# A two-layer hybrid decoder trunk: work between weight units issued behind the weight splits, and one tile per PSUM bank

## The chip, the cores and the metric

The kernel runs on one core of one Trainium2 chip. The metric is device time in microseconds of one execution of the whole kernel, the median of three runs. Float32 is the type of all data; TensorE works on pairs of reduced-precision float32 operands, as told below.

## What is computed

Two layers act on a sequence of 256 positions with 2048 channels. The first has a combined input projection that feeds a state-space mixer (a causal convolution of four taps, a chunked scan over 32 heads) and a block attention with 16 heads; the second has a diagonal complex state-space mixer with a gated linear unit. Cut to the parts that matter here:

```python
# layer 0
z, xbc, dt, q, k, v, gate = jnp.split(x @ w_in, SPLITS0, axis=-1)
xbc = jax.nn.silu(causal_depthwise_conv(xbc, conv_w, conv_b))      # 4 taps
y   = ssd_chunked_scan(xh * dt[..., None], dt * a, b, c) + d_skip * xh
y_a = rms_norm(y * jax.nn.silu(z), norm_g)
y_b = moba_attention(rotary(q), rotary(k), v) * jax.nn.silu(gate)
h   = jnp.concatenate([y_a, y_b], axis=-1) @ w_out
# layer 1
u, gate = jnp.split(x @ w_in, 2, axis=-1)
y  = jax.nn.gelu(s5_ssm(u, ...))                                   # complex diagonal recurrence
ga, gb = jnp.split(y @ w_glu, 2, axis=-1)
h  = (ga * jax.nn.sigmoid(gb) * jax.nn.silu(gate)) @ w_out
# both layers
x  = layer_norm(alpha * x + h, g, b)
```

## The kernel before

**Weight units.** All weights are read from HBM as 432 units of 128 x 1024 float32 (512 KB each), in one order for the whole kernel. For each unit `split_to` loads `raw` on SyncE's queue (line 227), ScalarE copies it to the high part `wh` (line 230), and VectorE subtracts that from `raw` for the low part `wl` (line 232). These two instructions are called the split here. The pool that holds `raw`, `wh` and `wl` has four buffers of each, so the split of a unit can start when TensorE has done with the unit four places earlier. `product` calls `split_to(unit[0] + 3)` ahead of a unit's matmuls, so a split is traced three units ahead of its use.

**Products.** A product is eight units (sixteen for the output projection of layer 0), accumulated into two PSUM banks. Each float32 product is three matmuls: high by high, high by low, low by high. `wmm` (line 284) has the weights stationary and leaves a transposed result, 24 matmuls of 256 columns for a unit; `xmm` (line 271) has the activations stationary, 12 matmuls of 512 columns for a unit. `banks()` (line 261) makes one tile of 128 x 2 x 512 that spans both banks, under one of two tags in turn; `Pair` is a list of the two halves that also keeps the whole as `both`. So the banks of a product are used again two products later. In the last unit of a product the first bank is finished before the second.

**Jobs.** What isn't a matmul by weights is cut into small functions. `jobs` holds those that follow a product at once (they read its banks), `back` a long list that is spread over many products. `pump` runs behind each unit's matmuls: it takes as many of `jobs` as are needed to be through by the end of the product, and those of `back` that are due by a rate. `drain` and `finish` run all that is left. Jobs issue on ScalarE, VectorE, TensorE and GpSimd as they need.

**Order on the engines.** The kernel's text gives a trace order only. A scheduler with a model of time then puts the instructions of every engine into a fixed order: at each step an engine takes the instruction with the earliest place in the trace among those that are ready. On the chip each engine runs its own queue strictly in that order and waits at the head of it. A job that was traced much later can so stand ahead of work that was traced earlier, if it was ready sooner in that model. `tc.issue_after(ins)` adds an edge that keeps what is traced inside it, on the engine of `ins`, behind `ins` in that engine's queue. It is an edge of order only, with no wait for `ins` to end. In the kernel before, it is used at two places: `y_split` (line 181) and the steps of the norm between the layers (lines 1002 and 1023).

**Jobs that the prediction follows.**
- `conv_jobs` (line 492): after a product that is to be convolved, four jobs `tap(f)`. Each is one ScalarE instruction (line 498) and three dependent VectorE instructions (line 501) that read the product's bank `f // 2`; a fifth job is a Silu (line 506).
- `trig_job` and `table_job` (lines 544 and 571): about 70 small VectorE instructions that prepare the coefficients of layer 1, traced in the product ahead of the second convolved product of the x columns. `phasor_job` (line 610) works on GpSimd.
- `block_jobs` (line 633): `bars`, `efs`, `pes` and `mts` for each of 16 blocks of layer 1, members of `back`, traced during the attention and the output projection. `bars` issues a load of `bc` on SyncE's queue (line 639) and begins with lines 645 to 651 on VectorE; `efs` has lines 665 to 675.
- `rope_jobs` (line 832): per bank one ScalarE copy (line 838) and VectorE products (lines 839 to 841).
- `product_apart` (line 323): the last product of a layer. Its last units are first accumulated into bank 0 alone, then `after` queues the jobs that read bank 0 (`res0`, line 960, or `res1`, line 1248), then the same units are accumulated into bank 1.
- `ssm(b)` (line 1079): for each of 16 blocks `enc` (TensorE), `rec1` (VectorE, lines 1113 to 1121), `rec2` (VectorE, a scan at line 1128 to line 1131), `dec` (TensorE, lines 1144 and 1148) and `act` (ScalarE), one stage in each step of `back`.
- `gate` (line 1212) in the gated linear unit and the Silu at line 1198, which read both banks by one instruction through `both`.

Of the kernel before, what the change touches and what calls it, by code (L numbers as in the profile page):

```python
# [9 lines left out]
F32 = mybir.dt.float32  # L10
F32R = mybir.dt.float32r
AF = mybir.ActivationFunctionType
OP = mybir.AluOpType
# [3 lines left out]
P = 128  # L17
# [17 lines left out]

SLOT = np.array([[8 * (q // 4) + 4 * (q % 2) + 2 * ((q // 2 % 2) ^ h) + q // 2 % 2 for q in range(64)] for h in range(2)])
GORDER = [16 * h + p + 8 * i for h in range(8) for p in range(8) for i in range(2)]

class Pair(list):
    def __init__(self, both, parts):  # L40
        super().__init__(parts)
        self.both = both


CONST = {}
PARAM = {}
# [118 lines left out]
def trunk(tc, io, out):  # L165
    nc = tc.nc
    V, A, G, T = nc.vector, nc.scalar, nc.gpsimd, nc.tensor
    count = [0]

    def nm(s):  # L170
        count[0] += 1
        return f"{s}_{count[0]}"

    with ExitStack() as top:
# [4 lines left out]
        main = enter(tc.tile_pool(name="main", bufs=1, space=PSUM))  # L179
# [18 lines left out]
        def big(tag, shape, dt=F32):  # L198
            return slot.tile(shape, dt, tag=tag, name=nm(tag))
# [4 lines left out]
        ready = {}  # L204
        nsplit = [0]
        early = {}
        last = {}
        keep = [None, range(0)]

        def split_to(i):  # L210
            while nsplit[0] <= min(i, len(units) - 1):
                n = nsplit[0]
                if n in early:
                    early.pop(n)()
                raw = st.tile([P, UK, 512], F32, tag="raw", name=nm("raw"))
                if n == 0:
                    wh = st.tile([P, UK, 512], F32R, tag="wh", name=nm("wh"))
                    wl = st.tile([P, UK, 512], F32R, tag="wl", name=nm("wl"))
                    for k in range(UK):
                        xpart(k)  # L220
                        nc.sync.dma_start(raw[:, k, :], units[n][:, k * 512 : k * 512 + 512])
                        A.activation(wh[:, k, :], raw[:, k, :], AF.Copy)
                        V.tensor_tensor(wl[:, k, :], raw[:, k, :], wh[:, k, :].bitcast(F32), op=OP.subtract)
                    ready[n] = (wh, wl)
                    nsplit[0] += 1
                    continue
                nc.sync.dma_start(raw.rearrange("p k n -> p (k n)"), units[n])
                pool, th, tl = (keep[0], f"wh{n % 8}", f"wl{n % 8}") if n in keep[1] else (st, "wh", "wl")
                wh = pool.tile([P, UK, 512], F32R, tag=th, name=nm("wh"))
                last["a"] = A.activation(wh, raw, AF.Copy)  # L230
                wl = pool.tile([P, UK, 512], F32R, tag=tl, name=nm("wl"))
                last["v"] = V.tensor_tensor(wl, raw, wh.bitcast(F32), op=OP.subtract)  # L232
                ready[n] = (wh, wl)
                nsplit[0] += 1

        jobs = deque()
        back = deque()
        goal = [0, 0.0]
        unit = [0]
        turnno = [0]  # L240

        def pump(left):
            n = -(-len(jobs) // max(left, 1))
            for _ in range(n):
                jobs.popleft()()
            if back:
                goal[1] += len(back) / max(goal[0] - unit[0], 1)
            while back and goal[1] >= 1.0:
                back.popleft()()
                goal[1] -= 1.0  # L250

        def drain():
            while jobs:
                jobs.popleft()()

        def finish():
            while back:
                back.popleft()()
            goal[1] = 0.0

        def banks():
            turnno[0] += 1
            both = main.tile([P, 2, 512], F32, tag=f"m{turnno[0] % 2}", name=nm("main"))
            return Pair(both, [both[:, o, :] for o in range(2)])

        def xmm(ps, o, wpair, j, hk, start, stop):
            (xh, xl), k = hk
# [20 lines left out]
        def product(kind, hl, nu=CU, prelude=None):  # L288
            ps = banks()
            for u in range(nu):  # L290
                if prelude:
                    prelude(u)
                split_to(unit[0] + 3)
                wpair = ready.pop(unit[0])
                if kind == "w":
                    wmm(ps, u, nu, hl, wpair)
                else:
                    last = u == nu - 1
                    steps = [(j, o) for o in range(2) for j in range(UK)] if last else [(j, o) for j in range(UK) for o in range(2)]
                    for j, o in steps:  # L300
                        xmm(ps, o, wpair, j, hl(u * UK + j), u == 0 and j == 0, last and j == UK - 1)
                unit[0] += 1
                pump(nu - 1 - u)
            return ps
# [68 lines left out]
        with ExitStack() as l0:  # L373
# [3 lines left out]
            def a4(shape, dt=F32):  # L377
                return wk.tile(shape, dt, tag="a4", bufs=6, name=nm("a4"))
# [22 lines left out]
            def xpart(k):  # L401
                xr = a4([P, S])
                nc.sync.dma_start(xr, io["xt"][:, k, :])
                A.activation(xh[:, k, :], xr, AF.Copy)
                V.tensor_tensor(xl[:, k, :], xr, xh[:, k, :].bitcast(F32), op=OP.subtract)
# [104 lines left out]
            ps = product("w", xhl)  # L510
# [3 lines left out]
            ps = product("w", xhl)  # L514
# [217 lines left out]
            for j in range(4):  # L732
                ps = product("w", xhl)
# [84 lines left out]
            for j in range(4):  # L818
                ps = product("w", xhl)
                for i in range(2):  # L820
                    fs = slice(4 * j + 2 * i, 4 * j + 2 * i + 2)
# [85 lines left out]
            for g in range(4):  # L907
                ps = product("w", xhl)
                qT = a4([P, 4, S])
                rope_jobs(ps, qT)  # L910
                ps = product("w", xhl)
                kT = a4([P, 4, S])
                rope_jobs(ps, kT)
                ps = product("x", xhl)
                v = a4([P, 2, 512])
# [8 lines left out]
                ps = product("w", xhl)  # L924
# [38 lines left out]
            ps = product("x", mixhl, 2 * CU, prelude=lambda u: drain() if u == 4 else None)  # L963
            x1[0] = big("D", [P, 2, D])
            jobs.append(lambda ps=ps: res0(a4([P, 2, 512]), ps, 0, (0, 1)))
            for j in range(1, 3):
                ps = product("x", mixhl, 2 * CU)
# [76 lines left out]
        with ExitStack() as l1:  # L1044
# [8 lines left out]
            y5 = {}  # L1053
# [121 lines left out]
            def y_split(j):  # L1175
                if j == 0:
                    y5["h"] = big("A", [P, KT, S], F32R)
                    y5["l"] = big("B", [P, KT, S], F32R)
                yt = y5[j]
                fs = slice(4 * j, 4 * j + 4)  # L1180
                with tc.issue_after(last["a"].ins), tc.issue_after(last["v"].ins):
                    A.activation(y5["h"][:, fs, :], yt, AF.Copy)
                    V.tensor_tensor(y5["l"][:, fs, :], yt, y5["h"][:, fs, :].bitcast(F32), op=OP.subtract)

            for b in range(16):
                ssm(b)
# [5 lines left out]
            sg1 = wk.tile([P, 2, D], F32, tag="sg1", bufs=1, name="sg1")  # L1192
            for j in range(8):
                ps = product("w" if j < 4 else "x", x1hl) if j else first1
                if j < 4:
                    jobs.append(lambda ps=ps, j=j: u_store(ps, j))
                else:
                    jobs.append(lambda ps=ps, j=j: A.activation(sg1[:, :, 512 * j - 2048 : 512 * j - 1536], ps.both, AF.Silu))
                if j == 0:
                    back.extend([lambda fs=fs: [f() for f in fs] for t, fs in sorted(steps.items())])  # L1200
                    goal[0] = unit[0] + 7*CU+10
# [7 lines left out]
            def glu_jobs(ps, j):  # L1209
                d = {}  # L1210

                def gate():
                    sb = w1("gt", [P, 2, 256])
                    A.activation(sb, ps.both[:, :, 256:512], AF.Sigmoid)
                    t1 = d["t"] = w1("p1", [P, 2, 256])
                    V.tensor_tensor(t1, ps.both[:, :, 0:256], sb, op=OP.mult)
                    V.tensor_tensor(t1, t1, sg1[:, :, 256 * j : 256 * j + 256], op=OP.mult)

                def turn():
                    px = sp.tile([P, 2, 512], F32, tag=("enc", "dec")[j % 2], name=nm("turn"))[:, 0, :]  # L1220
                    transpose4(px, [d["t"][:, o, f * P : f * P + P] for f in range(2) for o in range(2)])
                    pv = px.rearrange("p (f s c) -> p f s c", f=2, s=4)
                    ho, lo = (y[:, 2 * j : 2 * j + 2, :].rearrange("p f (c s) -> p f s c", s=4) for y in (y2h, y2l))
                    A.activation(ho, pv, AF.Copy)
                    V.tensor_tensor(lo, pv, ho.bitcast(F32), op=OP.subtract)

                rest = lambda: None
                jobs.extend([gate, rest, rest, turn])
# [5 lines left out]
            for j in range(2, 8):  # L1234
                ps = product("x", y5hl)
# [3 lines left out]
        with ExitStack() as l2:  # L1239
# [11 lines left out]
            for j in range(3):  # L1251
                ps = product("x", y2hl, prelude=lambda u: split_to(unit[0] + 3 + u) if j == 2 else None) if j else first2
# [45 lines left out]
```

## Time and profile before

| | us |
|---|---|
| median of three runs (lowest, highest) | 1376.59 (1375.08, 1376.98) |
| the profiled execution, its time | 1375.91 |
| its span, first to last instruction | 1374.1 |
| mean granted TensorE clock in it | 0.992 of full speed |

The lines of the profile show one execution. Times are in microseconds from the start of the span unless marked ns. PE is TensorE's matmuls, DVE VectorE, ACT ScalarE, POOL GpSimd, SP SyncE. A line such as `L284` is a line of the kernel. In a timeline a row gives the start, the duration, the engine, the line, the operation, the tile written and the tiles read with their shapes, the number of instructions merged into the row, and in brackets how long the engine sat idle before it and which instruction ended that. In the answer on waits a row reads: who waited, for whom, the total, how many times, the longest. In the answer on windows a row gives a stretch, its length, the busy time of each engine with its instructions, the granted clock, the share of DMA time and GB/s.

### The profile page before, as it was taken

The numbers are of one execution on the slowest core, as the hardware profiler recorded it, in microseconds if no ns is written. First come the engines' busy times: TensorE is split into PE (matmuls) and PEld (weight loads), VectorE is DVE, ScalarE is ACT, GpSimd is POOL, SyncE is SP. The second block draws the span as 40 slices with busy tenths as digits, with TensorE's granted clock in tenths as the row PEclk, the third lists the DMA queues.
The fourth block names the chain that finished last, engine by engine and source line by source line (L and its number), as shares of the span: only waits on it lengthen the run. The fifth ranks groups of instructions, "written<-read, shape, count | busy, mean of one in ns | idle before, by whom it ended". The sixth has DMA issues, their size and how long they took to land.

```text
span 1374.1 us, 24912 instructions
## 1 busy us (share of the span) xinstructions
PE 1346.6 (98%) x9944; PEld 1214.5 (88%) x9944; DVE 979.9 (71%) x1548; ACT 673.7 (49%) x856; POOL 307.1 (22%) x457
## 2 busy tenths in 40 slices
PE   9996999999999999999999999899999999999996
PEld 9996999998999999999988888799977788888885
DVE  5789768888666679688768855748888846555555
ACT  5563557765554454454464434344344545444441
POOL 0157787833002002002000000023343200000001
PEclk9998999999999999999999999999999999999998
DMA  8554766555556656646756678387988766666761
GB/s 307 175 162 132 229 195 189 162 181 154 168 162 193 217 164 213 223 150 220 243 175 222 218 219 302 120 305 237 297 278 306 216 211 190 185 192 190 247 216 74
DMA packets 79204, 283.01 MB, mean 206 GB/s; under 512 B 9840, under 2 KB 10480, under 8 KB 78576
## 3 DMA queue, kind: packets, MB, share of 16 engines
q1 hardware_dynamic: 68112, 239.33, 55.4%
q0 software_dynamic: 10400, 40.90, 9.0%
q8 instruction: 78, 1.28, 0.4%
q10 hardware_dynamic: 576, 1.18, 0.2%
q14 instruction: 38, 0.31, 0.1%
HBM read 260.41 MB, written 20.97 MB: 205 GB/s over the span
## 4 chain that ended last, share of the span: by engine, by line
PE 91%; DVE 3%; DMA 2%; POOL 2%; ACT 1%; issue 1%; POOLq 0%; SPq 0%; DVEq 0%; ACTq 0%
PE main L271 42%; PE main L284 41%; DVE wl L232 1%; PE aux L351 1%; PE enc L1103 1%; PE aux L781 1%; DMA raw<-in_wo 1%; PE aux L687 1%; DMA raw<-in_wi 1%; PE aux L359 1%; DMA xr<-in_xn 1%; PE dec L1148 1%; POOL ew L461 1%; PE aux L683 1%; PE aux L861 1%
## 5 line engine op out<-in xcount | busy, mean ns | idle before, releaser
L232 DVE TENSOR_TENSOR wl<-raw,wh 128x1024 fp32r<-128x1024 f32 x431 | 540.7, 1259 | 281.2 <-ACT wh L230 275.2
L230 ACT ACTIVATE wh<-raw 128x1024 fp32r<-128x1024 f32 x431 | 455.4, 1059 | 549.4 <-PE main L271 272.5
L284 PE MATMUL main<-A,wh 128*128 128x256 f32 x1408 | 404.0, 287 | 10.3 <-DVE a L501 10.3
L284 PE MATMUL main<-A,wl 128*128 128x256 f32 x1408 | 400.8, 285 | 0.0
L284 PE MATMUL main<-B,wh 128*128 128x256 f32 x1408 | 400.2, 284 | 0.0
L284 PEld LDWEIGHTS main<-A,wh 128*128 128x128 f32 x1408 | 271.5, 193 | 11.2 <-issue 10.7
L284 PEld LDWEIGHTS main<-B,wh 128*128 128x128 f32 x1408 | 271.5, 193 | 0.3
L284 PEld LDWEIGHTS main<-A,wl 128*128 128x128 f32 x1408 | 271.5, 193 | 0.1
L271 PE MATMUL main<-wh,A 128*128 128x512 f32 x512 | 201.2, 393 | 1.7 <-DVE D L960 1.7
L271 PE MATMUL main<-wl,A 128*128 128x512 f32 x512 | 200.0, 391 | 0.0
L271 PE MATMUL main<-wh,B 128*128 128x512 f32 x512 | 199.6, 390 | 0.0
L271 PE MATMUL main<-wh,C 128*128 128x512 f32 x384 | 152.7, 398 | 0.8 <-DVE D L1248 0.8
L271 PE MATMUL main<-wl,C 128*128 128x512 f32 x384 | 149.9, 390 | 0.0
L271 PE MATMUL main<-wh,F 128*128 128x512 f32 x384 | 149.7, 390 | 0.0
L271 PEld LDWEIGHTS main<-wh,A 128*128 128x128 f32 x512 | 96.1, 188 | 22.2 <-DVE D L960 2.1
L271 PEld LDWEIGHTS main<-wh,B 128*128 128x128 f32 x512 | 96.1, 188 | 20.0
L271 PEld LDWEIGHTS main<-wl,A 128*128 128x128 f32 x512 | 96.2, 188 | 19.2
L271 PEld LDWEIGHTS main<-wh,C 128*128 128x128 f32 x384 | 72.1, 188 | 16.8 <-DVE D L1248 1.2
L271 PEld LDWEIGHTS main<-wh,F 128*128 128x128 f32 x384 | 72.1, 188 | 15.2
L271 PEld LDWEIGHTS main<-wl,C 128*128 128x128 f32 x384 | 72.1, 188 | 14.2
L284 PE MATMUL main<-C,wh 128*128 128x256 f32 x256 | 74.1, 290 | 0.7 <-ACT C L1014 0.7
L284 PE MATMUL main<-F,wh 128*128 128x256 f32 x256 | 73.5, 287 | 0.3 <-DVE F L1015 0.3
(281 smaller groups left out, 1575.6 us busy)
## 6 DMA issues: line engine op xcount, KB each, us to landing
raw<-in_wi SPq DMA_DIRECT2D x271, 512.0 KB, 4.2
raw<-in_wo SPq DMA_DIRECT2D x96, 512.0 KB, 4.2
raw<-in_wglu SPq DMA_DIRECT2D x64, 512.0 KB, 3.7
wt<-wb POOLq DMA_DIRECT2D x16, 896.0 KB, 7.7
wb<-ob POOLq DMA_DIRECT2D x16, 512.0 KB, 5.8
bc<-in_s5bc SPq DMA_DIRECT2D x16, 256.0 KB, 4.3
wb<-F POOLq DMA_DIRECT2D x16, 256.0 KB, 4.0
wb<-om POOLq DMA_DIRECT2D x16, 128.0 KB, 4.3
```

Of the source, the lines that this page charges most:

```text
L230: last["a"] = A.activation(wh, raw, AF.Copy)
L232: last["v"] = V.tensor_tensor(wl, raw, wh.bitcast(F32), op=OP.subtract)
L271: T.matmul(ps[o], l[:, k, sl], r[:, j, :], start=start and i == 0, stop=stop and i == 2)
L284: T.matmul(pv[o // 2][:, o % 2, :], l[:, j, sl], r[:, k, :], start=first and i == 0 and o % 2 == 0, stop=end and i == 2 and o % 2 == 1, sk ...
L351: T.transpose(dst[:, i * P : i * P + P], s, ident)
L359: T.matmul(px[:64, 0:64], idle, idle, start=i == 0, stop=i == n - 1)
L461: G.tensor_scalar(pl, pl, 1.0 / (2 * k + 1), None, op0=OP.add)
L683: T.transpose(pe[:, a * P : a * P + P], ev[:, a, :], ident)
L687: T.matmul(pk[at : at + 64, a * 16 : a * 16 + 16], ev[:, a, 64 * i : 64 * i + 64], cv[:, a, i, :], start=True, stop=True)
L781: T.matmul(yo, xs[:, 0, xc], df[:, i, 0:256], start=True, stop=False)
L861: T.matmul(px[:, 128:384], qT[:, h, P:S], kT[:, h, :], start=True, stop=True)
L1103: T.matmul(px[64 * at : 64 * at + 64, i, r * 128 + q * 64 : r * 128 + q * 64 + 64], wt[64 * i : 64 * i + 64, a * P + 64 * r : a * P + 64 * ...
```

## The change

Every job is now run through a new function `run`, which opens an `issue_after` edge to the two split instructions of one unit before it calls the job. At the time of `pump` behind a unit, `unit[0]` is already that unit plus one, so the split is that of the third unit ahead of the one whose matmuls were just traced, or the last one split if there is none so far ahead. All ScalarE and VectorE instructions of the job stand behind it in their queues. Instructions on TensorE, GpSimd and SyncE get no edge. The special edge in `y_split` goes. `split_to` keeps the two instructions of every unit in `splits`.

The second part: `banks()` makes two tiles of one bank each in place of one tile of two banks, and the class `Pair` goes. The two kinds of instruction that read both banks at once are therefore cut in two: the Silu of the gate columns in layer 1 (four products) and the Sigmoid and the first product of `gate` (eight products).

```diff
-                last["a"] = A.activation(wh, raw, AF.Copy)
+                high = A.activation(wh, raw, AF.Copy)
                 wl = pool.tile([P, UK, 512], F32R, tag=tl, name=nm("wl"))
-                last["v"] = V.tensor_tensor(wl, raw, wh.bitcast(F32), op=OP.subtract)
+                splits[n] = (high, V.tensor_tensor(wl, raw, wh.bitcast(F32), op=OP.subtract))
...
+        def run(job):
+            with ExitStack() as pin:
+                for ins in splits.get(min(unit[0] + 2, nsplit[0] - 1), ()):
+                    pin.enter_context(tc.issue_after(ins.ins))
+                job()
+
         def pump(left):
             n = -(-len(jobs) // max(left, 1))
             for _ in range(n):
-                jobs.popleft()()
+                run(jobs.popleft())
...
-                back.popleft()()
+                run(back.popleft())
...
         def banks():
             turnno[0] += 1
-            both = main.tile([P, 2, 512], F32, tag=f"m{turnno[0] % 2}", name=nm("main"))
-            return Pair(both, [both[:, o, :] for o in range(2)])
+            return [main.tile([P, 512], F32, tag=f"m{turnno[0] % 2}{o}", name=nm("main")) for o in range(2)]
...
-                with tc.issue_after(last["a"].ins), tc.issue_after(last["v"].ins):
-                    A.activation(y5["h"][:, fs, :], yt, AF.Copy)
-                    V.tensor_tensor(y5["l"][:, fs, :], yt, y5["h"][:, fs, :].bitcast(F32), op=OP.subtract)
+                A.activation(y5["h"][:, fs, :], yt, AF.Copy)
+                V.tensor_tensor(y5["l"][:, fs, :], yt, y5["h"][:, fs, :].bitcast(F32), op=OP.subtract)
...
-                    jobs.append(lambda ps=ps, j=j: A.activation(sg1[:, :, 512 * j - 2048 : 512 * j - 1536], ps.both, AF.Silu))
+                    jobs.append(lambda ps=ps, j=j: [A.activation(sg1[:, t, 512 * j - 2048 : 512 * j - 1536], ps[t], AF.Silu) for t in range(2)])
...
-                    A.activation(sb, ps.both[:, :, 256:512], AF.Sigmoid)
                     t1 = d["t"] = w1("p1", [P, 2, 256])
-                    V.tensor_tensor(t1, ps.both[:, :, 0:256], sb, op=OP.mult)
+                    for t in range(2):
+                        A.activation(sb[:, t, :], ps[t][:, 256:512], AF.Sigmoid)
+                    for t in range(2):
+                        V.tensor_tensor(t1[:, t, :], ps[t][:, 0:256], sb[:, t, :], op=OP.mult)
                     V.tensor_tensor(t1, t1, sg1[:, :, 256 * j : 256 * j + 256], op=OP.mult)
```

`drain` and `finish` go through `run` in the same way.

More of the change, by code (lines that the diff above doesn't have):

```diff
@@ L37 @@
 GORDER = [16 * h + p + 8 * i for h in range(8) for p in range(8) for i in range(2)]
[L39 to L42, printed above, removed]
 CONST = {}
@@ L206, in trunk @@
         early = {}
-        last = {}
+        splits = {}
         keep = [None, range(0)]
@@ L253, in drain @@
             while jobs:
-                jobs.popleft()()
+                run(jobs.popleft())
         def finish():
             while back:
-                back.popleft()()
+                run(back.popleft())
             goal[1] = 0.0
```

## The prediction

> **What bounds the kernel now.** I read the shares of busy time first, then TensorE's waits, then the stretch in which its longest wait lies.
>
> ```profile
> span 1374.1 us, 24912 instructions
> ...
> PE 1346.6 (98%) x9944; PEld 1214.5 (88%) x9944; DVE 979.9 (71%) x1548; ACT 673.7 (49%) x856; POOL 307.1 (22%) x457
> ```
>
> TensorE is the bound, and it has 1374.1 - 1346.6 = 27.5 us without work. A change that adds and removes no matmul can win only from these and from a lowered clock, or lose by adding to them. So the answer on TensorE's waits comes next.
>
> ```profile
> PE main L284 <- DVE a L501: 10.3, 1, 10.3
> PE main L271 <- DVE D L960: 1.7, 1, 1.7
> ...
> PE main L271 <- DVE D L1248: 0.8, 1, 0.8
> ```
>
> One wait of 10.3 us is the largest item. No wait for a split (`wl` L232) is in that answer: no split is late for TensorE today, so putting splits first wins nothing by itself. The long wait, in the timeline and in windows of all engines (PE, PEld, DVE, ACT, POOL busy; then the clock):
>
> ```profile
> 109.24 0.28 PE L284 MATMUL main<-A,wl 128*128 128x256 f32 x1
> 119.86 0.55 PE L284 MATMUL main<-A,wh 128*128 128x256 f32 x1 [10.34 <-DVE a L501]
> ```
>
> ```profile
> 92.00:109.20 17.20, 17.20 (x146) 17.20 (x145) 16.18 (x41) 9.89 (x15) 10.59 (x20) 1.00 0.51 154
> 109.20:119.90 10.70, 0.36 (x4) 0.19 (x2) 10.70 (x24) 1.62 (x3) 7.31 (x11) 0.73 0.52 161
> 119.90:130.20 10.30, 10.30 (x70) 10.30 (x71) 9.70 (x28) 5.71 (x7) 9.17 (x24) 0.79 0.09 38
> 130.20:148.00 17.80, 17.80 (x152) 17.80 (x151) 15.36 (x31) 8.96 (x11) 13.65 (x26) 1.00 0.63 193
> ```
>
> At 109.24 the third convolved product of the x columns cannot begin, since VectorE still reads the banks of the first (the last `tap`). VectorE is full: 10.70 of 10.70 us. The clock is low behind the wait too: 0.79 over 10.3 us costs 10.3 x 0.21 = 2.2 us. Wait and clock together: 12.5 us.
>
> **The ties.** What VectorE does in that wait:
>
> ```profile
> 108.71 0.73 DVE L645 TENSOR_TENSOR bb<-bc,wri 128x128 f32<-128x128 f32 x1
> 109.37 0.61 DVE L647 SCALAR_TENSOR_TENSOR bb<-bc,consts,wri 128x128 f32<-128x128 f32 x1
> ...
> 115.01 0.28 DVE L646 TENSOR_TENSOR tm<-bc,wri 128x128 f32<-128x128 f32 x1
> 115.22 0.34 DVE L648 SCALAR_TENSOR_TENSOR tm<-bc,consts,wri 128x128 f32<-128x128 f32 x1
> 115.48 0.47 DVE L501 SCALAR_TENSOR_TENSOR a<-main,params,a 128x255 f32<-128x255 f32 x1
> ...
> 118.47 0.60 DVE L665 TENSOR_TENSOR et<-bb,lam 128x128 f32<-128x128 f32 x2
> ...
> 119.03 0.38 DVE L666 TENSOR_TENSOR tm<-bb,lam 128x128 f32<-128x128 f32 x1
> 119.25 0.46 DVE L501 SCALAR_TENSOR_TENSOR a<-main,params,a 128x253 f32<-128x253 f32 x1
> ...
> 144.91 0.36 DVE L646 TENSOR_TENSOR tm<-bc,wri 128x128 f32<-128x128 f32 x1 [2.40 <-DMA bc<-in_s5bc]
> ```
>
> L645 to L666 are `bars` and `efs` of the first S5 block. They were traced during the attention, long after the taps, and stand here because their inputs were ready. Behind the tie they follow a split of the attention and leave this stretch. The six rows shown ahead of the last tap are 0.73 + 0.61 + 0.28 + 0.34 + 0.60 + 0.38 = 2.9 us. In the whole stretch (windows of the instructions on tile `bc`, then on `et`, two sets without overlap):
>
> ```profile
> 92.00:148.00 56.00, 4.92 (x12) 0.91 0.47 147
> ```
>
> ```profile
> 92.00:148.00 56.00, 0.00 (x0) 0.00 (x0) 1.70 (x5) 0.91 0.47 147
> ```
>
> So 6.6 us of VectorE's work goes, and the 2.40 us at 144.91 in which a block's instruction at the head of the queue waited for its DMA. Both come back during the attention and the output projection, beside matmuls, with no bank to hold up. The load of `bc` has no edge (SyncE), but its buffer comes free with `efs`, so it moves with the ties; raw loads stand behind it on that queue, with four buffers of raw weights as cover.
>
> **The banks.** The waits of 1.7 and 0.8 us are in `product_apart`: the matmul that waits writes bank 1, the VectorE instruction that it waits for (L960, L1248) reads bank 0. They share only the two-bank tile. With a tile for each bank both waits go: 1.7 + 0.8 = 2.5 us. What follows hangs on the end of bank 1's matmuls and moves up with them. The same dependency strings the taps together:
>
> ```profile
> 97.92 0.56 ACT L498 ACTIVATE a<-main,params 128x256 f32<-128x256 f32 x1 [1.15 <-DVE a L501]
> ...
> 104.35 0.56 ACT L498 ACTIVATE a<-main,params 128x256 f32<-128x256 f32 x1 [2.44 <-DVE a L501]
> ...
> 110.87 0.56 ACT L498 ACTIVATE a<-main,params 128x256 f32<-128x256 f32 x1 [3.20 <-DVE a L501]
> ```
>
> These begin taps 1, 2 and 3. Tap 2 reads the other bank and yet waits 2.44 us for tap 1's VectorE work. With two tiles taps 2 and 3 can run beside tap 1, and can start up to 104.35 - 97.92 = 6.4 us earlier.
>
> How much of the 12.5 us goes? At least 2.9 (the rows ahead of the last tap, clock still lowered); at most all 12.5. For the value I count VectorE's load. It was busy 16.18 + 10.70 + 9.70 + 15.36 = 51.9 us from 92 to 148; less 6.6 that is 45.3. TensorE without wait and low clock takes 56 - 12.5 = 43.5 us for its part. VectorE is then 1.8 us short, and 17.20 - 16.18 = 1.0 us of idle in the first window waits for ScalarE and stays: 2.8. Since the order in the queue won't be the best, I take a stall of 4 us, by the next taps or by a split that is now late, in one piece or several. In this trace the clock fell about 5 us into the wait (0.73 over 10.7 us is 5.8 us at half speed), so 4 us leaves it up. Win: 12.5 - 4 = 8.5 us.
>
> By "What's actually happening" in "TensorE: Matmul & The Clock Gate" of the Trainium skill the clock halves after one idle window of about 3.4 us; by that, an unbroken 4 us could still cost what it costs now, and the win would be 6.3.
>
> **What is added.** One instruction on both banks becomes two, by these groups (count | busy us, mean ns):
>
> ```profile
> L1198 ACT ACTIVATE sg<-main 128x1024 f32<-128x1024 f32 x4 | 4.1, 1028 | 0.0
> L1214 ACT ACTIVATE gt<-main 128x512 f32<-128x512 f32 x8 | 4.6, 580 | 0.0
> L1216 DVE TENSOR_TENSOR p<-main,gt 128x512 f32<-128x512 f32 x8 | 5.5, 684 | 0.7 <-ACT gt L1214 0.7
> ...
> L498 ACT ACTIVATE a<-main,params 128x256 f32<-128x256 f32 x24 | 13.4, 558 | 20.6 <-DVE a L501 20.5
> L501 DVE SCALAR_TENSOR_TENSOR a<-main,params,a 128x255 f32<-128x255 f32 (+2 forms) x72 | 34.1, 474 | 1.6 <-ACT a L498 0.5
> ```
>
> Silu: 4 x (2 x 0.580 - 1.028) = 0.5 us. Sigmoid: 8 x (2 x 0.558 - 0.580) = 4.3 us. Product: 8 x (2 x 0.474 - 0.684) = 2.1 us. Beside them:
>
> ```profile
> 1150.00:1285.00 135.00, 135.00 (x610) 111.74 (x610) 73.25 (x67) 60.20 (x61) 1.09 (x2) 1.00 0.65 204
> ```
>
> VectorE and ScalarE are about half idle there while matmuls fill all 135 us, so the cost is nothing; without that cover it is 6.9 us.
>
> **The sum.** 2.5 + 8.5 = 11.0 us. The profiled execution's 1375.91 would be 1364.9; it lies 0.7 under the median 1376.59, so I forecast 1376.59 - 11.0 = 1365.6 us. Its own range, the stall that is left between 1 and 8 us: 1362 to 1370.
>
> **What the ties can cost.** A tied job stands behind a split that waits for a weight buffer, and so do all jobs behind it. The nearest chain back to TensorE is in layer 1, where `dec` needs `rec2`:
>
> ```profile
> 961.34 1.27 DVE L1128 TENSOR_TENSOR_SCAN gt<-rt,p 128x256 f32<-128x256 f32 x2
> ...
> 965.50 0.42 DVE L1131 SCALAR_TENSOR_TENSOR gt<-p,p 128x256 f32<-128x256 f32 x1
> ...
> 969.13 1.23 DVE L232 TENSOR_TENSOR wl<-raw,wh 128x1024 fp32r<-128x1024 f32 x1 [2.08 <-ACT wh L230]
> ...
> 972.72 1.28 DVE L1113 TENSOR_TENSOR p<-enc,wt 128x512 f32<-128x512 f32 x2
> ```
>
> ```profile
> 974.19 0.34 PE L1144 MATMUL dec<-um,wt 64*64 64x64 f32 x8
> ```
>
> Counted by units, this `rec2` belongs behind the split at 969.13: it starts 9 us later. Today 974.19 - 965.92 = 8.3 us lie between its end and `dec`. Nearly all goes, but `dec` has no edge and is placed where its input is ready, between other matmuls; so I price it at nothing. If its place in TensorE's queue is too early, each block waits.
>
> **The rivals.**
>
> *Slower: the recurrence arrives late.* If the next block's `rec1` (972.72) also goes first, `rec2` begins at 969.13 + 1.2 + 2.1 = 972.4 and ends about 3.5 us of its own work later, 975.9: `dec` would wait 1.7 us. At all 16 blocks that is 27 us; at half of them, 13.6, for slacks and shifts differ: 1365.6 + 13.6 = 1379. It decides from the point at which `rec2` moves more than 8.3 us. For it: VectorE is in order, and 8.3 us is about the shift. Against it: TensorE shows no such wait today.
>
> *Faster by less: VectorE is slowed, not crowded.* It works beside GpSimd's `phasor_job` here, and its small instructions are stretched:
>
> ```profile
> 129.76 1.11 DVE L606 TENSOR_TENSOR a<-lap 128x64 f32<-128x64 f32 x1
> ...
> 135.57 0.27 DVE L606 TENSOR_TENSOR a<-lap 128x64 f32<-128x64 f32 x1
> ```
>
> The same instruction takes 1.11 us at one time and 0.27 at another. If that sets the pace, what the ties clear away is filled by waiting, and only the 2.9 us and the banks' 2.5 are won: 1376.6 - 5.4 = 1371.2. "Who interferes with whom" in "SBUF — State Buffer" of the Trainium skill says that a VectorE instruction with two SBUF inputs and a GpSimd instruction that reads SBUF block each other; by it the stretch stays, since the change moves nothing on GpSimd.
>
> *Nothing.* Dependencies are kept per bank already, and the queues' order is what the model of time makes of VectorE's load either way: 1376.6. Against it stands the wait of tap 2 on tap 1.
>
> **Chances.** Forecast 0.50, faster by less 0.17, nothing 0.08, slower 0.25. So faster by over 0.2% (2.8 us, about what a measurement of this kernel can tell from no change) 0.67, within it 0.08, slower 0.25. The range 1361 to 1381 leaves out the upper half of the slower case and the last of the win.
>
> **What would show it.** Right: no wait for L960 or L1248 in TensorE's waits; no L645 before 400 us; the wait for L501 under 5 us and the clock at 1.00 from 110 to 130 us; tap 2 not waiting for tap 1. Wrong: the wait for L501 still near 10 us, new waits of TensorE for L1131 or L232, or any of several microseconds elsewhere.

## The result and the profile after

| | before | after |
|---|---|---|
| median of 20 runs, us | 1376.64 | 1373.97 |
| lowest and highest | 1374.97, 1379.20 | 1368.98, 1376.19 |
| profiled execution: time, span | 1375.91, 1374.1 | 1374.45, 1372.7 |

The ratio after to before is 0.9979, with a 95% interval of 0.9973 to 0.9985. The kernel is faster by 2.7 us, a quarter of the 11.0 us forecast, and its runs spread over 7.2 us where those of before spread over 4.2. The span and the shares of busy time of the changed kernel:

```profile
span 1372.7 us, 24925 instructions
...
PE 1351.4 (98%) x9944; PEld 1216.5 (89%) x9944; DVE 980.6 (71%) x1556; ACT 673.0 (49%) x868; POOL 296.9 (22%) x457
```

TensorE has 21.3 us without work in place of 27.5, but is busy 4.8 us longer with the same matmuls, though the mean granted clock of the span is 0.992 in both executions. The answer on TensorE's waits (who waited, for whom, total, times, longest):

```profile
PE dec L1147 <- DVE gt L1129: 3.7, 1, 3.7
PE aux L350 <- DVE D L1005: 1.4, 1, 1.4
...
PE main L283 <- DVE a L500: 0.9, 1, 0.9
PE dec L1143 <- ACT ys L1153: 0.9, 1, 0.9
...
PE enc L1102 <- DMA um<-ud: 0.5, 1, 0.5
PE enc L1102 <- issue: 0.4, 1, 0.4
```

The wait for the taps fell from 10.3 to 0.9 us, those for the two residuals (1.7 and 0.8) are gone, and `dec` and `enc` wait where they didn't before. The windows of the stretch with the taps and of the gated linear unit, columns as before:

```profile
109.20:119.90 10.70, 9.81 (x82) 9.61 (x81) 10.48 (x21) 7.14 (x9) 6.37 (x7) 1.00 0.69 202
119.90:130.20 10.30, 10.30 (x90) 10.30 (x89) 10.30 (x25) 4.80 (x7) 8.74 (x21) 1.00 0.67 204
...
1110.00:1285.00 175.00, 175.00 (x789) 144.84 (x788) 96.11 (x95) 80.61 (x89) 2.61 (x5) 1.00 0.66 205
```

The clock is whole through the taps, and the added instructions of the gated unit open no gap in 175 us of matmuls. Where the win went is read by comparing the start of the same weight unit in both traces, after minus before:

| start in before, us | after minus before, us | what lies ahead of it |
|---|---|---|
| 124.8 | -11.6 | the taps |
| 866.6 | -12.1 | the first residual |
| 923.3 | -10.9 | the start of layer 1 |
| 1008.7 | -3.7 | `dec` and the lowered clock |
| 1109.7 | -0.4 | the end of the recurrence |
| 1351.1 | -1.4 | the second residual |

So 12.1 us were won in layer 0, 1.2 of them went in the start of layer 1, and 10.5 were lost again between 923 and 1110 us, in the recurrence of layer 1. The timeline there, GpSimd's queue first, then ScalarE, VectorE and TensorE:

```profile
980.69 0.77 POOL L1058 DMA_DIRECT2D ud<-ut  x1 [0.50 <-ACT ut L1057]
...
990.41 0.75 POOL L1172 DMA_DIRECT2D ut<-yd  x1 [7.32 <-DMA ud<-ut]
...
998.15 1.06 ACT L1180 ACTIVATE A<-ut 128x1024 fp32r<-128x1024 f32 x1 [8.48 <-DMA ut<-yd]
...
991.27 1.26 DVE L1127 TENSOR_TENSOR_SCAN gt<-rt,p 128x256 f32<-128x256 f32 x2
999.24 1.23 DVE L1181 TENSOR_TENSOR B<-ut,A 128x1024 fp32r<-128x1024 f32 x1 [6.71 <-ACT A L1180]
1000.39 1.29 DVE L1114 TENSOR_TENSOR p<-gt,wt 128x512 f32<-128x512 f32 x2
...
1002.93 0.60 DVE L1129 TENSOR_TENSOR gt<-p,p 128x256 f32<-128x256 f32 x1
...
999.54 0.34 PE L1143 MATMUL dec<-um,wt 64*64 64x64 f32 x8 [0.86 <-ACT ys L1153]
1003.59 0.82 PE L1147 MATMUL dec<-gt,wt 64*64 64x63 f32 x16 [3.71 <-DVE gt L1129]
```

Read it from the top. The store of `u` still reads the one buffer `ut`; the load of the first quarter of `y` needs that buffer and is issued only at 990.41. `y_split` for it stands at the head of ScalarE's queue for 8.48 us and of VectorE's for 6.71 us. On VectorE it stands in the middle of `rec2`, between the scan (L1127) and the products (L1114), so the products and L1129 come late and `dec` waits 0.86 + 3.71 us. The same load was late before, as the same two queues show:

```profile
1004.74 1.06 ACT L1182 ACTIVATE A<-ut 128x1024 fp32r<-128x1024 f32 x1 [5.86 <-DMA ut<-yd]
...
999.79 0.61 DVE L1131 SCALAR_TENSOR_TENSOR gt<-p,p 128x256 f32<-128x256 f32 x1
1000.32 1.21 DVE L232 TENSOR_TENSOR wl<-raw,wh 128x1024 fp32r<-128x1024 f32 x1
1005.83 1.23 DVE L1183 TENSOR_TENSOR B<-ut,A 128x1024 fp32r<-128x1024 f32 x1 [4.30 <-ACT A L1182]
```

There `rec2` had ended (L1131 at 1000.4) before VectorE stood still for 4.30 us, and nobody waited. Behind the wait the clock is low (windows of the changed kernel):

```profile
990.00:1000.00 10.00, 9.02 (x75) 6.83 (x73) 3.29 (x5) 1.84 (x3) 4.16 (x7) 1.00 0.93 260
1000.00:1010.00 10.00, 6.41 (x55) 5.29 (x56) 8.10 (x12) 2.73 (x4) 3.81 (x7) 0.66 0.76 221
...
1003.59:1010.00 6.41, 6.41 (x55) 5.29 (x56) 4.51 (x7) 0.40 (x1) 0.56 (x1) 0.63 0.87 270
```

A low clock costs only where TensorE has work. That is from 1003.59 on, when the second wait of `dec` ends: 0.63 over 6.41 us, so 6.41 x 0.37 = 2.4 us. With the waits of `dec` (4.6) and of `enc` (0.9) 7.9 of the 10.5 us are named. The other 2.6 are no waits. What can be counted there in TensorE's queue: the matmuls of `dec` lay in 16 unbroken pieces between the weight matmuls before, one for each block, and lie in 23 after, since seven blocks are cut in two.

### The profile page after: what moved, and what is told of

Same layout as the page of the kernel before. It is cut to its first block, busy times and chain, and to the rows that moved or that the text cites. A ratio compares the mean times of both kernels' runs of the same rounds, so it can differ in the third digit from the quotient of the medians.

```text
span 1372.7 us, 24925 instructions
## 1 busy us (share of the span) xinstructions
PE 1351.4 (98%) x9944; PEld 1216.5 (89%) x9944; DVE 980.6 (71%) x1556; ACT 673.0 (49%) x868; POOL 296.9 (22%) x457
## 4 chain that ended last, share of the span: by engine, by line
PE 91%; DVE 3%; POOL 2%; DMA 2%; issue 1%; ACT 1%; POOLq 0%; ACTq 0%; DVEq 0%
PE main L270 44%; PE main L283 39%; PE aux L350 1%; DVE wl L226 1%; PE aux L780 1%; PE aux L686 1%; PE enc L1102 1%; PE dec L1147 1%; DMA um<-ud 1%; DMA ut<-yd 1%; PE aux L358 1%; POOL ew L460 1%; PE aux L892 1%; PE aux L682 1%; PE aux L860 1%
```

## The experiments

Two theories stood at the start. One, as the prediction had it: the ties clear the taps, the banks add 2.5 us, and something in the recurrence takes it back. The other: the banks do all of the good, the ties do the harm. Each run is compared with the kernel before, run beside it. The median of that kernel lay between 1375.63 and 1376.64 us in the different sets, so that medians of two sets can be compared to about 1 us.

| run | what it is | median, us | ratio to before (95%) |
|---|---|---|---|
| e1 | banks alone | 1365.82 | 0.9929 (0.9917 to 0.9942) |
| e2 | ties alone | 1385.19 | 1.0070 (1.0057 to 1.0082) |
| e3 | banks, ties up to layer 1's recurrence | 1364.85 | 0.9921 (0.9908 to 0.9935) |
| e4 | the change, `y_split` later | 1366.63 | 0.9934 (0.9921 to 0.9946) |
| e5 | the change, `rec2` without a tie | 1370.93 | 0.9965 (0.9951 to 0.9978) |
| e6 | the change, first load of `y` in own room | 1366.95 | 0.9931 (0.9919 to 0.9943) |
| e7 | banks, ties of the blocks alone | 1364.85 | 0.9915 (0.9902 to 0.9928) |
| e8 | e3, wide warm-up that reads tile C | 1369.72 | 0.9956 (0.9944 to 0.9968) |
| e9 | e3, wide warm-up that reads tile A | 1362.26 | 0.9899 (0.9883 to 0.9915) |
| e10 | e3, `dec` traced in two jobs | 1371.66 | 0.9967 (0.9955 to 0.9978) |

**e1: banks alone.** The kernel before, with these lines only:

```diff
-            both = main.tile([P, 2, 512], F32, tag=f"m{turnno[0] % 2}", name=nm("main"))
-            return Pair(both, [both[:, o, :] for o in range(2)])
+            return [main.tile([P, 512], F32, tag=f"m{turnno[0] % 2}{o}", name=nm("main")) for o in range(2)]
```

and the Silu, Sigmoid and product cut in two as in the change.

> The kernel before with one tile per bank and no ties. If the banks and the ties win apart from each other: the waits for L960 and L1248 (1.7 + 0.8 us) go, the wait of 10.3 us for the taps shrinks only by what taps 2 and 3 gain by starting ahead (estimate 3 to 7 us, with the lowered clock behind it), and nothing is lost in the recurrence: 1367 to 1374 us. If the ties alone clear the taps: 1374 us, with the wait near 10 us. If the banks alone clear them: 1363 to 1365 us, faster than the changed kernel.

It is 9.8 us faster than before and 8.2 us faster than the whole change by the medians; the time lies between the ranges of the first and the third expectation, nearer the third. The timeline of VectorE, then of ScalarE, and the window of the whole stretch:

```profile
105.01 0.47 DVE L494 SCALAR_TENSOR_TENSOR a<-main,params,a 128x253 f32<-128x253 f32 x1
...
109.87 0.28 DVE L638 TENSOR_TENSOR bb<-bc,wri 128x128 f32<-128x128 f32 x1
...
89.97 0.58 ACT L491 ACTIVATE a<-main,params 128x256 f32<-128x256 f32 x1
...
96.19 1.02 ACT L491 ACTIVATE a<-main,params 128x256 f32<-128x256 f32 x2 [1.54 <-DVE a L494]
```

```profile
92.00:148.00 56.00, 54.52 (x454) 54.11 (x453) 55.48 (x119) 27.51 (x35) 41.92 (x64) 1.00 0.55 170
```

L638 is the first instruction of `bars` (L645 before): the block's work still stands in this stretch, and VectorE is busy 55.48 of 56 us. Yet the last instruction of the last tap starts at 105.01, where it started at 119.25 before, and TensorE has no wait for a tap at all. The taps now run in two pairs: ScalarE begins the first tap of the second bank at 89.97, 0.6 us behind that of the first bank, and the other two together at 96.19. TensorE's largest wait is now this, for two splits:

```profile
PE main L277 <- DVE wl L226: 3.4, 2, 2.0
```

One of the two, 1.4 us, lies in this stretch. So a full VectorE costs TensorE little here; what let the wait grow to 10.3 us was the order that the shared tile forced on the taps. The recurrence loses nothing: no wait of `dec`, 16 pieces.

**e2: ties alone.** The changed kernel with the tile of two banks and the three single instructions put back.

```diff
-            return [main.tile([P, 512], F32, tag=f"m{turnno[0] % 2}{o}", name=nm("main")) for o in range(2)]
+            both = main.tile([P, 2, 512], F32, tag=f"m{turnno[0] % 2}", name=nm("main"))
+            return Pair(both, [both[:, o, :] for o in range(2)])
```

> The changed kernel with the tile of two banks put back. If the loss at the recurrence comes from the ties, it is here too: waits of dec for L1129 and L1153 near 998 us, TensorE some 10 us behind between 920 and 1110 us; the waits for the two residuals are back (2.5 us). If the ties alone clear the taps, 1375 to 1377 us; if the banks did, the wait for the taps is near 10 us again and the time is 1384 to 1388 us.

1385.19 us, 9.6 slower than before: the ties by themselves are a loss. TensorE's waits and the window of the taps:

```profile
PE main L290 <- DVE a L507: 6.5, 1, 6.5
PE dec L1154 <- DVE gt L1136: 3.7, 1, 3.7
PE main L277 <- DVE D L966: 2.2, 1, 2.2
PE dec L1150 <- ACT ys L1160: 2.0, 1, 2.0
```

```profile
92.00:148.00 56.00, 49.52 (x394) 49.35 (x394) 50.25 (x106) 28.40 (x38) 40.60 (x74) 0.94 0.54 168
```

The blocks' work has left the stretch (`bars` first runs at 424.5 us) and VectorE sits idle for 5.75 of 56 us, but TensorE still waits 6.5 us for a tap, where the expectation had near 10 for this case. Beside e1 this settles it: with the tile shared, an emptier VectorE takes 3.8 us off the wait and keeps the rest; with the tile split, a full one has none. The waits of `dec` are there without the banks, so they come from the ties.

**e3: no ties in the recurrence.** The changed kernel; the steps of `back` run untied from the start of layer 1, `y_split` alone keeps its tie there.

```diff
-                back.popleft()()
+                (run if tied[0] else lambda f: f())(back.popleft())
...
+                    tied[0] = False
```

> The changed kernel without the ties of the recurrence's steps in layer 1 (the attention's and the blocks' jobs keep theirs, and the split of y keeps its own). If the ties of the recurrence give back the win: no wait of dec over 1 us, the clock whole at 1000 us, some 8 to 10 us faster than the changed kernel, 1363 to 1366 us. If the 10 us behind come from the banks, or from another stretch (the coefficients of the blocks late in layer 1): no more than 2 us faster, 1372 to 1374 us.

1364.85 us; no wait of `dec` or `enc`, and TensorE keeps its lead of 10.7 us from 923 to 1110 us to within 0.1 us. The late load is still there, as in the kernel before:

```profile
993.62 1.06 ACT L1181 ACTIVATE A<-ut 128x1024 fp32r<-128x1024 f32 x1 [5.50 <-DMA ut<-yd]
...
989.24 0.41 DVE L1131 SCALAR_TENSOR_TENSOR gt<-p,p 128x256 f32<-128x256 f32 x1
989.58 1.21 DVE L226 TENSOR_TENSOR wl<-raw,wh 128x1024 fp32r<-128x1024 f32 x1
994.72 1.23 DVE L1182 TENSOR_TENSOR B<-ut,A 128x1024 fp32r<-128x1024 f32 x1 [3.93 <-ACT A L1181]
```

VectorE stands still for 3.93 us with `rec2` already done (L1131). All ties outside the recurrence together are worth 1.0 us against e1 by the medians; the intervals overlap, so this is not told apart from nothing. The two traces lean towards a gain: e1's 3.4 us of waits for splits aren't there in e3, and at the start of layer 1 TensorE is 2.1 us further in e3, though its clock was low for longer between the layers (a mean of 0.72 from 866 to 878 us in e3, 0.86 in e1). That is one execution of each.

**e4: the split of `y` later.** The changed kernel, the first three splits three steps later:

```diff
-                    at(2 * b + 8, lambda b=b: y_split(b // 4))
+                    at(2 * b + (8 if b == 15 else 11), lambda b=b: y_split(b // 4))
```

> The changed kernel with the first three splits of y traced three steps later, so that their loads have landed before the split stands at the head of the queue. If rec2 is late since it stands behind a split of y that waits for its load: the wait of 3.7 us of dec and the lowered clock behind it go, 6 to 7 us of the 10, 1366 to 1368 us. If rec2 is late because of the tie to the weight split alone: the waits of dec stay near 4 us, 1372 to 1375 us.

1366.63 us, inside the first theory's 1366 to 1368. The wait of `dec` and the lowered clock behind it are gone.

**e5: `rec2` without a tie.** The changed kernel, every other step tied:

```diff
-                    back.extend([lambda fs=fs: [f() for f in fs] for t, fs in sorted(steps.items())])
+                    back.extend([lambda fs=fs: [f() if f.__name__ == "rec2" else run(f) for f in fs] for t, fs in sorted(steps.items())])
...
+                    tied[0] = False
```

> The changed kernel with every tie kept but the one of rec2 (scan to the last product of the rotation). If dec waits since rec2 stands behind the split of y in VectorE's queue: rec2 runs ahead of it, no wait of dec over 1 us, the clock whole at 1000 us, 1364 to 1367 us. If the ties of the other steps (rec1, enc's successors, act) delay the recurrence as much: the wait of dec stays over 2 us and the time is 1369 to 1373 us.

1370.93 us, with runs from 1366.28 to 1374.01: the median lies in the second range, the runs reach into the first. The timeline of VectorE, in an execution that was the fastest of them:

```profile
989.30 1.27 DVE L1128 TENSOR_TENSOR_SCAN gt<-rt,p 128x256 f32<-128x256 f32 x2
994.69 1.23 DVE L1182 TENSOR_TENSOR B<-ut,A 128x1024 fp32r<-128x1024 f32 x1 [4.12 <-ACT A L1181]
995.83 1.29 DVE L1115 TENSOR_TENSOR p<-gt,wt 128x512 f32<-128x512 f32 x2
```

The split of `y` stands in the middle of `rec2` even so. So `rec2`'s own tie isn't needed to put it there. The likely reason is that with `rec1` tied `rec2` comes late enough for the split to slip between its instructions; no run frees `rec1` alone, so this is argued and not shown. `dec` waited 2.0 us in this execution. That the spread over 7.7 us comes from when the load lands was not measured run by run, but the runs in which no `dec` stands behind that load spread less: 1.9 us in e3, 0.9 in e4, 2.6 in e6.

**e6: the load of `y` earlier, nothing else.** The changed kernel; the first quarter of `y` goes into a part of `sg1` that is free until products 6 and 7 of the layer's input.

```diff
-                y5[j] = w1("ut", [P, 4, S], 1)
+                y5[j] = w1("ut", [P, 4, S], 1) if j else sg1[:, 1, 1024:2048].rearrange("p (f s) -> p f s", f=4)
```

> The changed kernel, all ties and places kept; only the first load of y goes into room that is free until the gate's later products, so that it needn't wait for the store that uses the shared buffer (7.3 us). If the load's late landing is the cause: the split of y finds its data, the wait of 3.7 us of dec and the lowered clock go, 1366 to 1368 us. If the place in the queue alone is the cause, or the load is late for another reason: the wait stays and the time is 1371 to 1374 us.

1366.95 us. GpSimd's queue and VectorE's:

```profile
982.40 0.76 POOL L1172 DMA_DIRECT2D sg<-yd  x1 [6.58 <-DVE gt L1127]
...
991.09 1.27 DVE L1127 TENSOR_TENSOR_SCAN gt<-rt,p 128x256 f32<-128x256 f32 x2
992.27 1.20 DVE L1181 TENSOR_TENSOR B<-sg,A 128x1024 fp32r<-128x1024 f32 x1
993.39 1.28 DVE L1114 TENSOR_TENSOR p<-gt,wt 128x512 f32<-128x512 f32 x2
```

This is the sharpest of the runs. The split stands where it stood in the changed kernel, between scan and products; but the load was issued at 982.40 in place of 990.41, the split waits for nothing, and the 7.0 us between e6 and the changed kernel's median are the price of that one wait at the head of a queue, with the lowered clock behind it. That fits the 4.6 us of waits and 2.4 us of low clock counted above. `dec` lies in 23 pieces here too, and the time stays about 2 us above e3: by the starts of weight units this run loses 3.6 us between 923 and 1110 us, 1.1 of them in waits of `enc`. The other 2.4 are nearly the 2.6 that were left without a wait in the changed kernel.

**e7: banks and the ties of the blocks alone.** As e1, with a tie on `bars`, `efs`, `pes` and `mts`; `tie` opens the same two edges as `run`:

```diff
-                return [bars, efs, pes, mts] if b % 2 else [bars, efs, pes]
+                return [tie(f) for f in ([bars, efs, pes, mts] if b % 2 else [bars, efs, pes])]
```

> The kernel before with one tile per bank and ties for the blocks' jobs of layer 1 alone (bars, efs, pes, mts). By the first run the banks alone leave 3.4 us of waits for wl and block instructions among the taps. If the block ties are what the rest of the ties is worth: no wait for wl, 1364 to 1365 us, as with all ties of layer 0. If it is the ties of the taps and coefficients: as with the banks alone, 1365 to 1367 us.

1364.85 us, as e3; one wait of 1.5 us for `wl` is left where there were two. The interval overlaps e1's, so that the block ties win anything stays unproven.

**e8 and e9: the warm-up between the layers.** e3 with wide matmuls in place of 60 narrow ones while the norm is computed; e8 takes its operand from tile C, e9 from tile A.

```diff
-            warm(WARM1)
+            px = aux()
+            hot = tailhl(0)[0][0]
+            for i in range(WARM1):
+                T.matmul(px[:, 0:256], hot[:, 0, 0:P], hot[:, 0, :], start=i == 0, stop=i == WARM1 - 1)
```

with `WARM1 = 40`, and `tailhl(16)` for e9.

> Ties in layer 0 only, as in the third run, and between the layers 40 matmuls of 128 columns of weights by 256 in place of 60 of 64 by 64 that keep TensorE busy until the norm is done. In the third run the granted clock falls at 868.6 us, 1.3 us after the last small matmul but 5 us after the last full one, for 6.8 us. If small matmuls don't hold the clock: it stays whole and 3 to 3.5 us go, 1361 to 1362 us. If the wait of 1.4 us behind them lowers it: no change, 1364 to 1366 us.

> As the run with 40 wide matmuls between the layers, but these read tile A, which nothing writes there (tile C, which the run before took, is written by the norm's steps, and TensorE's wait for the norm grew from 1.4 to 5.3 us). In that run the clock was whole until 3.6 us after the last wide matmul. If small matmuls don't hold the clock: it stays whole at the transition, 3 to 3.5 us less than with the ties of layer 0, 1361 to 1362 us. If the wait of about 1 us for the norm lowers it in any case: 1364 to 1366 us.

e8 lost 4.9 us by the medians: the norm's steps write tile C, had to wait for the warm-up to read it, and TensorE then waited 5.3 us for them. e9 took 1362.26 us, 2.6 less than e3 and 14.1 less than before: the fastest kernel here, 0.3 above the first range. Windows of 1 us at the transition, first e3, then e9:

```profile
868.00:869.00 1.00, 0.31 (x2) 0.31 (x3) 0.64 (x1) 0.00 (x0) 0.00 (x0) 0.80 0.00 0
869.00:870.00 1.00, 0.81 (x4) 0.41 (x2) 0.00 (x0) 0.15 (x1) 0.00 (x0) 0.50 0.00 0
```

```profile
868.00:869.00 1.00, 0.89 (x8) 0.62 (x6) 0.46 (x1) 0.00 (x0) 0.00 (x0) 1.00 0.00 0
869.00:870.00 1.00, 0.31 (x3) 0.14 (x2) 0.16 (x1) 0.60 (x1) 0.00 (x0) 1.00 0.00 0
```

The clock is 0.50 in e3 and 1.00 in e9 in the window at 869, though TensorE has less work there in e9. Two things differ, however: the wide matmuls ran for 5.0 us in place of 3.7, so that the wait of 1.4 us for the norm is gone as well. e9 alone doesn't tell which of them kept the clock; e8 helps, as told at the end.

**e10: `dec` in two jobs.** e3 with the two halves of `dec` as steps of their own:

```diff
+                at(t + 3.5, lambda: dec((1,)))
```

> Ties in layer 0 only, and dec of every block traced as two jobs, so that TensorE's queue has 32 pieces of dec between the matmuls of the weights in place of 16; the work is the same. In the third run a piece costs 0.28 us on entering and 0.15 on leaving beside 0.18 between two matmuls of the weights and 0.015 within dec, about 0.24 us for each. If the 2 us that are left to the runs with the split of y mended come from dec lying in 22 pieces: 16 x 0.24 = 3.8 us more than the third run, 1368 to 1369 us. If entering and leaving is covered: 1364 to 1366 us.

1371.66 us, 6.8 above e3 by the medians where 3.8 were expected. The queue has 32 pieces, and in the profile TensorE has new waits of 0.8 and 0.7 us in `enc`. Pieces cost time, then, but this run doesn't give their price cleanly: more steps in the same number of units also change the pace of the recurrence, and about 1.5 us have no name. The changed kernel has 7 pieces more than before (23, not the 22 of the expectation). They are worth 1.7 us by the price of 0.24 us in the expectation; with the 7.9 us above that makes 9.6 of the 10.5 us lost. That the pieces are the cause of this last part is likely, not shown.

## Where the prediction held and where it failed

**Banks, 2.5 us: right.** Both waits are gone, and the unit starts show 1.9 us won at the first residual and 0.9 at the second. At the first, 1.2 us went again into the start of layer 1, where the clock was low for longer: the window from 866 to 878 us of the changed kernel has a mean clock of 0.72, the one from 878 to 890 of the kernel before 0.86.

**Taps, 8.5 us with 4 us of the wait left: the term was undersized, and its reason was wrong.** 11.6 us went, with 0.9 us of the wait left: 9.4 of the wait and the 2.2 of the low clock behind it. The step that failed is "For the value I count VectorE's load". In e1 the load stayed and the wait went; in e2 the load went and 6.5 us of the wait stayed. The taps were a chain of four, each a ScalarE instruction and three VectorE instructions, run one after the other since all shared one tile. The prediction named this, that taps 2 and 3 "can start up to 104.35 - 97.92 = 6.4 us earlier", and gave it no term. Rows of the changed kernel, ScalarE, then VectorE, then TensorE:

```profile
95.44 0.55 ACT L497 ACTIVATE a<-main,params 128x256 f32<-128x256 f32 x1
...
97.60 0.56 ACT L497 ACTIVATE a<-main,params 128x256 f32<-128x256 f32 x1 [0.50 <-DVE a L500]
...
104.32 0.57 ACT L497 ACTIVATE a<-main,params 128x256 f32<-128x256 f32 x1 [2.53 <-DVE a L500]
...
112.64 0.47 DVE L500 SCALAR_TENSOR_TENSOR a<-main,params,a 128x253 f32<-128x253 f32 x1
...
113.16 0.39 PE L283 MATMUL main<-A,wh 128*128 128x256 f32 x1 [0.89 <-DVE a L500]
```

The rows don't name the taps, but the waits tell them apart. The one at 95.44 waits for no tap, while the first tap is still at work, so it is tap 2, on the other bank, 104.35 - 95.44 = 8.9 us earlier. The one at 97.60 starts as the first tap's last product ends: it is tap 1, on the same bank, where it was. Tap 3 follows tap 2, 110.87 - 104.32 = 6.6 us earlier, and its last product is 119.25 - 112.64 = 6.6 us earlier too. That is 6.6 of the 9.4 us. For the other 2.8 TensorE went on: its wait begins at 112.27 (113.16 - 0.89) in place of 109.52. From 109.23 on it ran 24 more matmuls, as many as bank 0 gets from two weight units, so most likely it filled the free bank while the other was still being read.

**The ties, credited with the departure of the blocks' work: that happened, and was worth nothing that could be told.** `bars` runs first at 416.1 us in the changed kernel, as forecast. With the tile shared it takes 3.8 us off the wait (e2); with the tile split there is no such wait left to shorten, and e3 and e7 lie within 1.0 us of e1.

**The added instructions, at nothing: right.** No wait of TensorE from 1110 to 1285 us.

**The ties' cost, at nothing: the step that spoiled the forecast.** It reads "`dec` has no edge and is placed where its input is ready, between other matmuls; so I price it at nothing." It measured 10.5 us: 4.6 of waits of `dec`, 2.4 of low clock behind them, 0.9 of waits of `enc`, and 2.6 without a wait, in a queue in which `dec` lies in more pieces. Waits of `enc` of this size stand in e1 (0.8) and e7 (1.1) too, without a tie on the recurrence, so those 0.9 needn't come from the ties. The rival "the recurrence arrives late" had the mechanism, `rec2` on VectorE later and `dec` waiting for it, but not the place: it looked for a loss in many blocks from the shift of `rec2` alone, while 7.0 us of the loss sit at one block, where the shift lets `y_split` in ahead. The row to find was in the trace of before: the 5.86 us in which ScalarE stood still for `ut<-yd`, and VectorE 4.30 us behind it. That idle time cost nothing only because of what stood ahead of it, and the change reorders exactly that. The special edge of `y_split` (line 1181 of the kernel before, not 181) goes with the change, and the prediction asked of no queue what the split itself waits for.

**The rival "VectorE is slowed, not crowded": fell.** Long splits are still there, 2.08 us at 137.65 in e1, with no wait for a tap and 1.4 us of one for a split.

**The clock.** An unbroken wait of 4 us at the taps, at which the prediction weighed the Trainium skill ("TensorE: Matmul & The Clock Gate", "What's actually happening"), did not occur. At `dec` two waits of 0.86 and 3.71 us with eight small matmuls between them were enough to lower the clock. It fell at about 1001.5 us, 1.6 us into the second wait and 2.8 us from the start of the first. That page's window of about 3.4 us is near in size, but neither wait had lasted as long by then, so this trace doesn't decide how the page counts broken idle time. The lowered clock cost 2.4 us there, on top of 4.6 us of waiting.

## What to carry to other kernels

Before pricing a change of order, list the instructions that already stand idle at the head of a queue for a DMA, even where no one waits today: each is harmless only by what stands ahead of it, and the change should be judged by what it moves behind them. When an engine seems too full to serve a chain in time, test the chain's dependencies first; here separate tiles for two banks did what emptying the engine couldn't. And run the parts of a change apart: one half of this one wins about 10 us, the other loses 8 to 10.

## What the runs showed of the hardware

Narrow matmuls between the layers didn't hold TensorE's clock. In e3, 60 matmuls of 128x64 by 64 columns ran from 863.55 to 867.26 us, and the clock fell at about 868.6, 1.3 us after the last of them. In e9, 40 matmuls of 128x128 by 256 columns ran from 863.37 to 868.41 us, and the clock stayed at 1.00 through a window in which TensorE was busy for 0.31 of 1 us. In e8, where TensorE then idled for 5.34 us, the clock stayed whole for about 3.6 us from the end of the last wide one, so the 1.3 us of idle time in e3 would not by themselves explain the fall there:

```profile
871.00:872.00 1.00, 0.00 (x0) 0.00 (x0) 0.93 (x3) 0.00 (x0) 0.00 (x0) 1.00 0.00 0
872.00:873.00 1.00, 0.00 (x0) 0.00 (x0) 0.96 (x4) 0.20 (x1) 0.00 (x0) 0.59 0.00 0
```

Going in and out of a group of small matmuls between large ones takes time of its own, by an estimate from the starts in e3 about 0.24 us (0.28 on entering and 0.15 on leaving, less 0.18 between two large ones and 0.015 within the group), which no wait shows.
